# One layer on one core: keys' and values' compression earlier, one more pair of chunks, fewer single chunks under the attentions

## The chip, the core and the metric

The kernel runs on one core of one Trainium2 chip. TensorE (PE) multiplies, its operands loaded by a weight load that overlaps the multiplication (PEld); VectorE (DVE) and ScalarE (ACT) do the elementwise work; GpSimd (POOL) issues some DMAs; SyncE (SP) issues most of them. Each engine takes its instructions in the order of the program. The metric is the device time of one execution: median 1623.22 us of 3 runs before the change (1623.16 to 1623.29).

## The reference

One decoder layer over 256 tokens of width 4096. What is computed, with the sizes:

```python
h = rmsnorm(x, norm_g)                 # 256 x 4096
proj = h @ w_in                        # 4096 x 13872: q,k,v,z of A (2048 each), q of B, 6 x 256 k/v of B, z of B, 48 gates
o_a = dilated_mixture(q_a, k_a, v_a)   # 16 heads of 128; three window/dilation patterns, merged
kc, vc = compress(kc), compress(vc)    # 15 blocks of 32 tokens: gelu((block + pe) @ w1) @ w2, w1 is 4096 x 256
o_b = nsa(q_b, kc, vc, ks, vs, kw, vw, gates)   # 16 heads: compressed, selected and windowed keys
y_a = rmsnorm(o_a, out_g_a) * silu(z_a)
y_b = rmsnorm(o_b, out_g_b) * silu(z_b)
out = rmsnorm(x + concat(y_a, y_b) @ w_out, final_g)
```

All inputs and outputs are 32-bit floats.

## The kernel before

**Products in three parts.** Each 32-bit operand is split into a high and a low part (`split_to`, L102: ACT rounds the high part at L105, DVE subtracts to get the low part at L106), and a product is three matmuls (`mm3`, L97: lines 98, 99, 100; the first needs only the high part of the streamed operand, the second its low part).

**Chunks.** The columns of `w_in` are worked off in chunks of 512. A chunk by itself (`add_chunk`, `run_stream`) is 32 slices of the contraction x 2 halves of the tokens x 3 = 192 matmuls that stream 512 columns; weights come in 8 units of 1 MB (4 for the narrow chunk of 256 columns, 8 smaller ones for that of 304), each split in two halves, and the name of the product is `acc`. **Pairs** (`run_pairs`) work two chunks at once. Of their 16 steps, 9 (`FAST`) form sums of blocks so that 7 block products do in place of 8, 7 do not: 9 x 21 + 7 x 24 = 357 matmuls for a pair in place of 384. The sums cost DVE more (L436 to L443). Results of a pair go through the tiles `parts` and GpSimd's DMAs to scratch tensors in DRAM, where some are accumulated; of the last pair they are kept on the chip and stored once.

**Stages, in order of time.** (1) The first stage: chunk 20 (keys and values to be compressed), the narrow chunk `kw` (256 columns) and the narrow chunk `vg` (304 columns), while `x` is loaded, split and its sums are formed. (2) Nine pairs, the ninth of them `sel` and `za0`; this stage is put out in the order in which it is written. (3) Single chunks: the gates z 1 to 3 of mixer A, 0 to 3 of mixer B, then the first chunk of the output projection; behind these 8 chunks run the compression of keys and of values, the attentions of mixers A and B, gating and the turning of y (`turn_y`). (4) Three pairs of the output projection, then the last chunk and the final norm.

**What sets the order in stages 1 and 3.** The work behind the chunks is a queue of generators, `tasks`. After each contraction slice `run_stream` adds `pace` to a credit (L368, times the chunk's width over 512, at most 2.0) and calls `advance()` once for each whole credit. `hooks[chunk, slice]` put tasks into the queue or issue loads. A scheduler then fixes the order of the instructions on each engine; `[waits ...]` in the pieces below are waits on another engine or a DMA.

**Compression** (`compress`, L833): 4 transposes `pt` (L840), an ACT copy `cT` (L841), two DVE additions `bt` (L853), the split `bhl`, then 32 matmuls `ph` (L875) of 512 columns over `w1` split in 8 groups of 1024 elements (`w1hl`), a small gelu, and the second product (`pk` for keys, `pv` for values).

**Attention of mixer A** (`attend_a`, L636), for each of 4 groups of 4 heads: scores `s`, ACT's exponential, DVE's weighting, transposes `pt`, split `pah`/`pal`, products with the values `po`.

Of the kernel before, what the change touches and what calls it, by code (L numbers as in the profile page):

```python
# [18 lines left out]
P = 128  # L19
# [64 lines left out]
def hybrid_trunk(ctx: ExitStack, tc: tile.TileContext, a: dict):  # L84
# [45 lines left out]
    x_raw = {}  # L130

    def load_xT(piece):
        q, half = divmod(piece, 2)
        if half == 0:
            xh.append(big.tile([P, QK, SEQ], F32R, name=f"xh{q}", tag="x", bufs=8))
            xl.append(big.tile([P, QK, SEQ], F32R, name=f"xl{q}", tag="x", bufs=8))
        t = x_raw[piece] = room["o"].tile([P, G4, SEQ], F32, name="xp", tag="o", bufs=8)
# [163 lines left out]
    def run_stream(begin=None, last=False, ordered=None):  # L301
# [7 lines left out]
        for i, (u, s) in enumerate(subs):  # L309
            while True:  # L310
                if n_st < len(units) and n_st <= u + (2 if i else 0):
# [3 lines left out]
                    if first and 8 <= n_st < 12:  # L315
                        load_x_nat(2 * (n_st - 8))
                        load_x_nat(2 * (n_st - 8) + 1)
# [41 lines left out]
            for j in range(n):  # L359
                k = k0 + n * s + j  # L360
                for m in range(NT):
                    h, l = lhs(k, m)
                    mm3(ps[m][:, :width], h, l, wh[:, j], wl[:, j], start=(k == 0), stop=(k == KT - 1))
                if k == KT - 1:
                    done(ps)
                if (c, k) in hooks:
                    hooks[c, k]()
                credit = min(credit + pace * width / CW, 2.0)  # L368
                while credit >= 1.0 and tasks:
                    credit -= 1.0  # L370
                    advance()
# [347 lines left out]
    waiting, finished, gated = [("a", 0)], set(), set()  # L719
# [9 lines left out]
    def mixer_done(which):  # L729
# [4 lines left out]
        todo = list(waiting)  # L734
        waiting.clear()
# [13 lines left out]
        while loaded:  # L749
            z, sz = loaded.popleft()  # L750
            for m in range(NT):
                nc.scalar.activation(sz[m], sz[m], AF.Silu, scale=rstd[:, m : m + 1] if z == ("a", 0) else 1.0)
# [80 lines left out]
    def compress(t, which):  # L833

        tT = room["zq"].tile([P, 2, NT, P], F32, name="cT", tag="zt", bufs=4)
# [20 lines left out]
        split_to(w2h, w2l, w2)  # L856
        yield
        ph = room["pso"].tile([4 * NC, 2, HID], F32, name="ph", tag="po")
        ready = {}
        for grp in range(9):  # L860
            if grp < 8:
                w = room["work"].tile([P, 2, 4, HID], F32R, name="w1hl", tag="n", bufs=2)
                hs = slice(4 * (grp % 2), 4 * (grp % 2) + 4)
                split_to(w[:, 0], w[:, 1], w1[4 * which + grp // 2][:, hs])
                ready[grp] = w
                if grp % 2 == 1:
                    load_w1(4 * which + grp // 2 + 3)
                if grp == 4 and which == 0:
                    load_small(1)
# [32 lines left out]
        if which == 0:  # L902
# [4 lines left out]
            kc = room["work"].tile([P, 2, CP], F32, name="kc", tag="kc", bufs=1)  # L907
# [3 lines left out]
        else:  # L911
            for g in range(2):
                wide = room["zq"].tile([P, 2, 3, Q], F32, name="wide", tag="zt", bufs=4)
# [3 lines left out]
                rh = room["work"].tile([P, 2, 3 * Q], F32R, name="rh", tag="pTh", bufs=2)  # L917
                rl = room["work"].tile([P, 2, 3 * Q], F32R, name="rl", tag="pTl", bufs=2)
# [360 lines left out]
    dcs.append(((21, 12), ("sel", "za0")))  # L1279
    ordered = ExitStack()  # L1280
# [45 lines left out]
    hooks[0, 3] = load_first  # L1326
    hooks[0, 8] = lambda: load_w1(2)
# [7 lines left out]
    hooks[n_in - 1, 16] = lambda: tasks.extend(turn_y("a", f) for f in range(8, 16, 2))  # L1335
# [121 lines left out]
```

## Time and profile before

| | us |
|---|---|
| median of 3 runs | 1623.22 |
| the profiled execution, its own time | 1622.32 |
| its span, first to last instruction | 1620.5 |
| PE busy in it | 1601.9 (99%) |
| DVE busy | 1368.8 (84%) |
| ACT busy | 994.6 (61%) |
| DMA moved, mean | 384.87 MB, 237 GB/s |

The profile's page says what share of the span each engine was busy, the chain of waits says what the last instruction was waiting for, step by step back; a table by stretch (start:end in us from the span's start) says the same of a stage, with the clock granted to TensorE (1.00 is its upper level of 2.4 GHz, 0.50 is 1.2 GHz) and the share of time in which the DMA engines moved data. Matmuls overlap, so what one costs is the distance of two starts and not the duration in a row.

### The profile page before, as it was taken

How to read it: one execution, taken by the hardware profiler on the slowest of the kernel's cores; microseconds unless marked ns; L12 is line 12 of the kernel's file. 1: busy time of each engine (PE TensorE's matmuls, PEld its weight loads, DVE VectorE, ACT ScalarE, POOL GpSimd, SP SyncE). 2: the span in 40 equal slices, each digit the busy share in tenths (PEclk: the TensorE clock that was granted, in tenths of full speed). 3: DMA queues.
4: the chain of work that ended last, by engine and by line, in shares of the span. 5: the costliest groups of instructions: out<-in, count | busy, mean ns of one | idle time of the engine just before them, and what ended most of it. 6: DMA issues, size and time to landing. Idle time of an engine off the chain costs nothing.

```text
span 1620.5 us, 20719 instructions
## 1 busy us (share of the span) xinstructions
PE 1601.9 (99%) x7685; PEld 1326.4 (82%) x7685; DVE 1368.8 (84%) x1596; ACT 994.6 (61%) x1242; POOL 142.6 (9%) x196
## 2 busy tenths in 40 slices
PE   9999999999999999999999999999999999999997
PEld 6998888888888888888887788888888887888887
DVE  8679989898999898989878877788788779989885
ACT  7755656565656565656546666766667655656553
POOL 0000212021212020202000000000000000202110
PEclk9999999999999999999999999999999999999999
DMA  8776888888888888888888555654345556988874
GB/s 336 268 250 208 261 264 260 254 260 266 256 270 259 253 263 262 264 249 262 251 312 306 179 190 193 233 174 143 117 144 189 179 194 211 261 252 259 280 299 169
DMA packets 104565, 384.87 MB, mean 237 GB/s; under 512 B 12496, under 2 KB 13136, under 8 KB 93072
## 3 DMA queue, kind: packets, MB, share of 16 engines
q1 hardware_dynamic: 81792, 332.42, 58.3%
q0 software_dynamic: 22240, 50.08, 13.8%
q8 instruction: 60, 0.98, 0.2%
q10 hardware_dynamic: 432, 1.05, 0.2%
q14 instruction: 41, 0.34, 0.1%
HBM read 334.69 MB, written 50.91 MB: 238 GB/s over the span
## 4 chain that ended last, share of the span: by engine, by line
PE 89%; DVE 6%; issue 2%; DMA 2%; ACT 1%; SPq 0%; ACTq 0%; POOLq 0%; POOL 0%; DVEq 0%
PE p L99 16%; PE p L100 16%; PE p L98 16%; PE acc L99 9%; PE acc L100 9%; PE acc L98 9%; PE e L100 2%; PE e L98 2%; PE e L99 2%; PE ph L875 1%; DVE wl L106 1%; PE pt L1056 1%; DVE bf L443 1%; DMA w<-in_w_in 1%; DVE bp L106 1%
## 5 line engine op out<-in xcount | busy, mean ns | idle before, releaser
L106 DVE TENSOR_TENSOR wl<-w,wh 128x1024 fp32r<-128x1024 f32 (+2 forms) x178 | 207.7, 1171 | 99.4 <-ACT wh L105 98.9
L105 ACT ACTIVATE wh<-w 128x1024 fp32r<-128x1024 f32 (+2 forms) x178 | 180.4, 1017 | 115.3 <-PE acc L100 99.9
L98 PE MATMUL acc<-wh,xh 128*128 128x512 f32 (+2 forms) x640 | 242.7, 379 | 0.6 <-ACT wh L105 0.6
L443 DVE TENSOR_TENSOR bf<-bt,bf 128x2048 fp32r<-128x2048 f32 x106 | 242.1, 2284 | 0.0
L99 PE MATMUL acc<-wl,xh 128*128 128x512 f32 (+2 forms) x640 | 239.7, 375 | 1.3 <-DVE wl L106 1.3
L100 PE MATMUL acc<-wh,xl 128*128 128x512 f32 (+2 forms) x640 | 239.2, 374 | 0.0
L106 DVE TENSOR_TENSOR bp<-bw,bp 128x2048 fp32r<-128x2048 f32 x72 | 164.8, 2288 | 69.5 <-ACT bp L105 69.5
L438 ACT ACTIVATE bf<-bt 128x1024 fp32r<-128x1024 f32 x106 | 112.4, 1060 | 163.0 <-DVE bt L436 162.6
L435 ACT ACTIVATE bf<-bw 128x1536 fp32r<-128x1536 f32 x106 | 157.7, 1488 | 72.2 <-DMA bw<-in_w_in 39.4
L105 ACT ACTIVATE bp<-bw 128x2048 fp32r<-128x2048 f32 x72 | 137.6, 1911 | 94.1 <-PE e L100 78.2
L442 DVE TENSOR_TENSOR bf<-bw,bf 128x1536 fp32r<-128x1536 f32 x106 | 185.6, 1751 | 0.0
L436 DVE TENSOR_TENSOR bt<-bw 128x1024 f32<-128x1024 f32 x106 | 129.5, 1222 | 12.6 <-DMA bw<-in_w_in 7.0
L441 ACT ACTIVATE bf<-bt 128x1024 fp32r<-128x1024 f32 x106 | 112.7, 1063 | 41.8 <-DVE bt L440 38.7
L99 PEld LDWEIGHTS acc<-wl,xh 128*128 128x128 f32 x640 | 120.6, 188 | 20.1 <-DVE wl L106 3.0
L100 PEld LDWEIGHTS acc<-wh,xl 128*128 128x128 f32 x640 | 120.2, 188 | 20.4
L98 PEld LDWEIGHTS acc<-wh,xh 128*128 128x128 f32 x640 | 120.4, 188 | 18.9 <-ACT wh L105 1.1
L98 PE MATMUL p<-bp,xh 128*128 128x512 f32 x324 | 126.0, 389 | 0.0
L99 PE MATMUL p<-bp,xh 128*128 128x512 f32 x324 | 126.0, 389 | 0.0
L100 PE MATMUL p<-bp,xl 128*128 128x512 f32 x324 | 126.0, 389 | 0.0
L99 PE MATMUL p<-bf,sum 128*128 128x512 f32 x320 | 124.7, 390 | 0.0
L98 PE MATMUL p<-bf,sum 128*128 128x512 f32 x320 | 124.6, 390 | 0.0
L100 PE MATMUL p<-bf,sum 128*128 128x512 f32 x320 | 124.5, 389 | 0.0
(327 smaller groups left out, 3373.8 us busy)
## 6 DMA issues: line engine op xcount, KB each, us to landing
bw<-in_w_in SPq DMA_DIRECT2D x288, 512.0 KB, 6.5
w<-in_w_in SPq DMA_DIRECT2D x60, 1024.0 KB, 5.2
bw<-in_w_out SPq DMA_DIRECT2D x96, 512.0 KB, 5.6
w<-in_w_out SPq DMA_DIRECT2D x16, 1024.0 KB, 5.5
scr_q<-parts POOLq DMA_DIRECT2D x30, 256.0 KB, 7.8
scr_k<-parts POOLq DMA_DIRECT2D x30, 256.0 KB, 7.7
scr_v<-parts POOLq DMA_DIRECT2D x30, 256.0 KB, 7.9
scr_qb<-parts POOLq DMA_DIRECT2D x30, 256.0 KB, 8.3
```

The costliest lines, as they stand in the source:

```text
L98: nc.tensor.matmul(out, lh, rh, start=start, stop=False)
L99: nc.tensor.matmul(out, lh, rl, start=False, stop=False)
L100: nc.tensor.matmul(out, ll, rh, start=False, stop=stop)
L105: nc.scalar.activation(h, src, AF.Copy)
L106: nc.vector.tensor_sub(l, src, h.bitcast(F32))
L435: nc.scalar.activation(h[:, :3], w[:, B22:], AF.Copy)
L436: nc.vector.tensor_tensor(t[:, T3 : T1 + 1], w[:, B22 : B11 + 1], w[:, B12 : B12 + 1].to_broadcast([P, 2, CW]), op=OP.subtract)
L438: nc.scalar.activation(h[:, 3:5], t[:, T3 : T1 + 1], AF.Copy)
L441: nc.scalar.activation(h[:, 5:], t[:, T2:], AF.Copy)
L442: nc.vector.tensor_sub(l[:, :3], w[:, B22:], h[:, :3].bitcast(F32))
L443: nc.vector.tensor_sub(l[:, 3:], t, h[:, 3:].bitcast(F32))
L875: nc.tensor.matmul(ph, both, w[:, :, j], start=l == 0, stop=l == CBL - 1)
```

## The change

Three things move together. (a) The compression of keys and values runs behind the two narrow chunks of the first stage in place of the first chunks of stage 3: the chunk's result `kvc` stays on the chip, the loads of `w1` and of `x` in its natural layout come earlier, `w1` is split in 16 groups of 512 elements in place of 8 of 1024, and its tiles share the buffers of `x`'s (`tag="xn"`, 4 of them). (b) The gates `za1` and `za2` become a tenth pair, so `sel` and `za0` go through the accumulating scratch and `za1`, `za2` are what the last pair keeps. (c) The attentions start at slice 6 of the first of 6 single chunks (5 gates and the first of the output projection) with `pace` 1.7 in place of 1.1 and 1.5, the credit's ceiling is 3.0, and `turn_y` of mixer A goes to the front of the queue.

```diff
@@ load_xT: one tile for two pieces, 4 buffers @@
+            x_pair[q] = room["o"].tile([P, 2, G4, SEQ], F32, name="xp", tag="o", bufs=4)
+        t = x_raw[piece] = x_pair[q][:, half]
@@ split_unit and run_stream: x in its natural layout two units earlier @@
-        if room["first"] and 8 <= u < 12:
-            square_x(2 * (u - 8) + half)
+        if room["first"] and 8 <= u < 10:
+            for i in range(2):
+                square_x(4 * (u - 8) + 2 * half + i)
-                    if first and 8 <= n_st < 12:
+                    if first and 6 <= n_st < 10:
-                credit = min(credit + pace * width / CW, 2.0)
+                credit = min(credit + pace * width / CW, 3.0)
@@ gates @@
+    paired = [("a", i) for i in range(3)]
-    waiting, finished, gated = [("a", 0)], set(), set()
+    waiting, finished, gated = list(paired), set(), set()
@@ compress: buffers, groups of half the size @@
-        tT = room["zq"].tile([P, 2, NT, P], F32, name="cT", tag="zt", bufs=4)
+        tT = room["work"].tile([P, 2, NT, P], F32, name="cT", tag="st")
-        for grp in range(9):
-            if grp < 8:
-                w = room["work"].tile([P, 2, 4, HID], F32R, name="w1hl", tag="n", bufs=2)
+        for grp in range(17):
+            if grp < 16:
+                w = spare([P, 2, 2, HID], F32R, "w1hl")
...
+            if grp % 2:
+                yield
...
-                rh = room["work"].tile([P, 2, 3 * Q], F32R, name="rh", tag="pTh", bufs=2)
-                rl = room["work"].tile([P, 2, 3 * Q], F32R, name="rl", tag="pTl", bufs=2)
+                r = spare([P, 2, 2, 3 * Q], F32R, "rhl")
@@ first stage @@
-    add_chunk([a["w_kw"][g] for g in range(4)], 2 * HD, x_lhs, evict_away("kw", 2 * HD), pace=0.8)
-    add_chunk([a["w_vg"][g] for g in range(8)], 2 * HD + NGATE, x_lhs, last_ps.extend, pace=0.8)
+    add_chunk([a["w_kw"][g] for g in range(4)], 2 * HD, x_lhs, evict_away("kw", 2 * HD), pace=1.4)
+    add_chunk([a["w_vg"][g] for g in range(8)], 2 * HD + NGATE, x_lhs, last_ps.extend, pace=1.6)
+
+    def start_compression():
+        kvc = room["ev"].tile([P, NT, CW], F32, name="kvc", tag="ev", bufs=3)
+        for m in range(NT):
+            nc.scalar.activation(kvc[:, m], first_ps[m], AF.Copy, scale=rstd[:, m : m + 1])
+        tasks.extend([compress(kvc, 0), compress(kvc, 1)])
-    hooks[1, 26] = token_rms
-    hooks[1, 28] = lambda: evict_away("kvc")(first_ps)
+    for k, i in ((2, 0), (6, 1), (10, 2)):
+        hooks[1, k] = lambda i=i: load_w1(i)
+    hooks[1, 4] = lambda: load_small(0)
+    hooks[1, 14] = token_rms
+    hooks[1, 16] = start_compression
@@ pairs and stage 3 @@
     dcs.append(((21, 12), ("sel", "za0")))
+    dcs.append(((13, 14), ("za1", "za2")))
-        tasks.extend([compress(t, 0), compress(t, 1)] + [attend_a(hg) for hg in range(4)] + [mixer_done("a"), start_b()]
+        tasks.extend([attend_a(hg) for hg in range(4)] + [mixer_done("a"), start_b()]
-    hooks[0, 10] = attentions
-    z_chunks = [("a", 12, i) for i in range(1, 4)] + [("b", 22, i) for i in range(4)]
+    hooks[0, 6] = attentions
+    z_chunks = [("a", 12, 3)] + [("b", 22, i) for i in range(4)]
-        add_chunk(w_chunk(c + i), CW, x_lhs, gate_z(which, i), pace=1.5 if chunks else 1.1)
+        add_chunk(w_chunk(c + i), CW, x_lhs, gate_z(which, i), pace=1.7)
-    hooks[n_in - 1, 8] = lambda: tasks.extend(turn_y("a", f) for f in range(0, 8, 2))
+    hooks[n_in - 1, 8] = lambda: tasks.extendleft(turn_y("a", f) for f in range(0, 8, 2))
```

**First place: the start of the values' compression.** On DVE before, in stage 3 (names: `bt` block sums, `bhl` their split, `wl` low parts of a chunk's weights, `w1hl` split `w1`):

```order
L853 TENSOR_TENSOR bt<-cT,pe 128x480 x2
L106 TENSOR_TENSOR wl<-w,wh 128x1024
L106 TENSOR_TENSOR bhl<-bt,bhl 128x32x30
L570 TENSOR_SCALAR fetched<-fetched,rstd 128x512 x2
L106 TENSOR_TENSOR wl<-w,wh 128x1024
L106 TENSOR_TENSOR w1hl<-w_6013,w1hl 128x1024 x2
```

And now, behind the chunk `vg`:

```order
L858 TENSOR_TENSOR bt<-cT,pe 128x480 x2
L106 TENSOR_TENSOR w2hl<-w_792,w2hl 128x256
L106 TENSOR_TENSOR w1hl<-w_867,w1hl 128x512 x2
L106 TENSOR_TENSOR bhl<-bt,bhl 128x32x30
L106 TENSOR_TENSOR wl<-w,wh 128x608 x2
L106 TENSOR_TENSOR w1hl<-w_867,w1hl 128x512 x2
```

The split of `bhl` now stands behind three splits of compression weights, and the chunk's own low parts stand behind it. On PE at the same place, the last rows between the transposes `pt` and the first `ph` after the change:

```order
L100 MATMUL acc<-wh,xl_109 128x304
L98 MATMUL acc<-wh,xh_108 128x304
L99 MATMUL acc<-wl,xh_108 128x304
L100 MATMUL acc<-wh,xl_109 128x304
L98 MATMUL acc<-wh,xh_170 128x304 x2
L880 MATMUL ph<-w1hl,bhl 60x512 x4
L99 MATMUL acc<-wl,xh_170 128x304
```

Between the 4 transposes `pt` and the first `ph` there stand 14 matmuls of 304 columns now, and 22 of 512 columns before; for the keys it is 46 of 256 columns now.

**Second place: the first pair's weights on SP.** Before (names: `w` units of `vg`, `bw` raw blocks of the pairs, `scr` scratch):

```order
L255 DMA w<-in_w_vg 128x1216 [waits DMAHW3_49,DVE_49]
L255 DMA w<-in_w_vg 128x1216 [waits DMAHW5_49,DVE_49]
L428 DMA bw_1150<-in_w_in 128x1024 [waits DMAHW1_49]
L429 DMA bw_1150<-in_w_in 128x1024
L428 DMA bw_1151<-in_w_in 128x1024
L429 DMA bw_1151<-in_w_in 128x1024 [waits DMAHW4_49]
```

And now:

```order
L828 DMA w_1121<-in_cmp_v_w 128x2048 [waits DVE_49]
L256 DMA w<-in_w_vg 128x1216 [waits DMAHW2_49,DMAHW6_49,DVE_49,Activation_49]
L256 DMA w<-in_w_vg 128x1216 [waits DMAHW7_49,DMAHW3_49,DVE_49]
L430 DMA bw_1451<-in_w_in 128x1024 [waits DMAHW4_49,DVE_49,PE_49]
L431 DMA bw_1451<-in_w_in 128x1024
L430 DMA bw_1452<-in_w_in 128x1024 [waits Pool_49]
```

The first load of the pairs waits for PE and DVE now: its place in the memory was the last `rhl` of the values' compression, and what it waits for is the last `pv` matmul and that tile's split. Behind that `pv` there stand 55 matmuls of `vg`.

**Third place: turning y of mixer A on PE.** Before, in the last gate chunk, the 4 turns (4 transposes each) stand in this way:

```order
L783 MATMUL pt<-ident,o_a_6482 128x128 x8
L98 MATMUL acc<-wh,xh_168 128x512
L99 MATMUL acc<-wl,xh_168 128x512
L100 MATMUL acc<-wh,xl_169 128x512
L98 MATMUL acc<-wh,xh_168 128x512
L99 MATMUL acc<-wl,xh_168 128x512
L100 MATMUL acc<-wh,xl_169 128x512
L783 MATMUL pt<-ident,o_a_6482 128x128 x4
```

And now, inside the last head group of mixer B:

```order
L1063 MATMUL pt<-ident,nb 128x128 x4
L786 MATMUL pt<-ident,o_a_6745 128x128 x4
L99 MATMUL acc<-wl,xh_170 128x512
L100 MATMUL acc<-wh,xl_171 128x512
L1082 MATMUL po<-pbh,vc_75 128x512
L786 MATMUL pt<-ident,o_a_6745 128x128 x12
L98 MATMUL po<-pbh,vB 128x512
L1063 MATMUL pt<-ident,nb 128x128 x4
```

Three turns follow each other with nothing between, on the three banks of `pt`.

## Rows read from the trace of the kernel before

**Rows 1.** The page: busy time of each engine; shares of the chain of waits.
```profile
PE 1601.9 (99%) x7685; PEld 1326.4 (82%) x7685; DVE 1368.8 (84%) x1596; ACT 994.6 (61%) x1242; POOL 142.6 (9%) x196
PE 89%; DVE 6%; issue 2%; DMA 2%; ACT 1%; SPq 0%; ACTq 0%; POOLq 0%; POOL 0%; DVEq 0%
```

**Rows 2.** Busy time by stretch: chunk 20, kw, vg, first pair, mixer A, later.
```profile
core 0: us, PE busy (x) PEld busy (x) DVE busy (x) ACT busy (x) POOL busy (x), PEclk, DMA share, GB/s
7.20:53.60 46.40, 45.79 (x192) 35.96 (x193) 44.99 (x89) 39.18 (x70) 0.00 (x0) 1.00 0.93 359
53.60:76.10 22.50, 22.50 (x193) 22.49 (x192) 12.45 (x19) 16.12 (x25) 0.70 (x1) 1.00 0.67 240
76.10:103.00 26.90, 26.90 (x194) 26.90 (x193) 13.36 (x16) 14.39 (x19) 0.00 (x0) 1.00 0.71 242
103.00:184.00 81.00, 81.00 (x359) 67.02 (x358) 75.24 (x54) 49.07 (x43) 2.78 (x5) 1.00 0.67 225
943.50:975.90 32.40, 31.49 (x176) 26.41 (x174) 25.00 (x58) 21.63 (x40) 0.00 (x0) 1.00 0.55 191
1010.00:1220.00 210.00, 209.19 (x1093) 171.04 (x1092) 171.37 (x417) 139.65 (x304) 4.40 (x10) 1.00 0.46 160
```

**Rows 3.** PE in order of time: first matmuls of the pairs and of stage 3.
```profile
103.03 0.40 PE L98 MATMUL p<-bf,xh 128*128 128x512 f32 x1
...
832.44 0.39 PE L98 MATMUL acc<-wh,xh 128*128 128x512 f32 x1
```

**Rows 4.** PE's waits: total us, times, longest us.
```profile
PE s L98 <- DVE pal L106: 2.8, 4, 1.1
PE acc L99 <- DVE wl L106: 1.3, 2, 0.7
```

**Rows 5.** The values' compression before, on PE, ACT and DVE (start us, us).
```profile
877.09 0.27 PE L840 MATMUL pt<-ident,fetched 128*128 128x128 f32 x1
...
877.73 0.60 ACT L841 ACTIVATE cT<-pt 128x512 f32<-128x512 f32 x1 [0.94 <-PE pt L840]
...
880.32 1.03 ACT L105 ACTIVATE bhl<-bt 128x960 fp32r<-128x960 f32 x1
...
878.36 1.93 DVE L853 TENSOR_TENSOR bt<-cT,pe 128x480 f32<-128x480 f32 x2 [0.37 <-ACT cT L841]
...
881.42 1.15 DVE L106 TENSOR_TENSOR bhl<-bt,bhl 128x960 fp32r<-128x960 f32 x1
...
882.72 1.11 PE L875 MATMUL ph<-w1hl,bhl 128*60 128x512 f32 x4
```

**Rows 6.** Splits of 512 and 256 elements on DVE (start us, us).
```profile
31.56 0.68 DVE L106 TENSOR_TENSOR sum<-st,sum 128x512 fp32r<-128x512 f32 x1
...
834.97 0.42 DVE L106 TENSOR_TENSOR w2l<-w,w2h 128x256 fp32r<-128x256 f32 x1 [1.65 <-ACT w2h L105]
```

**Rows 7.** The first pair's weights: issue, us to landing, first split.
```profile
90.06 0.42 SPq L428 DMA_DIRECT2D bw<-in_w_in  x1
90.53 0.43 SPq L429 DMA_DIRECT2D bw<-in_w_in  x1
...
bw<-in_w_in SPq DMA_DIRECT2D x2, 512.0 KB, 5.4
...
98.81 1.90 ACT L105 ACTIVATE bf<-bw 128x2048 fp32r<-128x2048 f32 x1
...
100.74 2.29 DVE L106 TENSOR_TENSOR bf<-bw,bf 128x2048 fp32r<-128x2048 f32 x1 [1.01 <-ACT bf L105]
```

**Rows 8.** ACT's copies of turned y: ns min/median/max.
```profile
L787 ACT ACTIVATE o_a<-pt,g_out x16: 466/484/511, 1232.9 to 1250.6; 128x256 f32<-128x256 f32 x16
```

**Rows 9.** The end of the span by stretch; the warm-up matmuls at its start.
```profile
1604.00:1613.00 9.00, 5.54 (x47) 5.34 (x45) 2.68 (x9) 1.67 (x3) 0.55 (x1) 1.00 0.31 123
1614.00:1620.00 6.00, 0.00 (x0) 0.00 (x0) 0.00 (x0) 0.00 (x0) 0.00 (x0) 0.50 0.68 267
...
1.26 5.30 PE L297 MATMUL warm<-idle 128*128 128x512 bf16 x13 [1.26 <-DVE idle L294]
```

More of the change, by code (lines that the diff above doesn't have):

```diff
@@ L128, in hybrid_trunk @@
     xh, xl = [], []
-    x_raw = {}
+    x_raw, x_pair = {}, {}
     def load_xT(piece):
@@ L314, in run_stream @@
                     stage_unit(n_st)
[L315 to L317 removed]
+                    if first and 6 <= n_st < 10:
+                        load_x_nat(2 * (n_st - 6))
+                        load_x_nat(2 * (n_st - 6) + 1)
                     n_st += 1
@@ L733, in mixer_done @@
         loaded = deque()
-        todo = list(waiting)
-        waiting.clear()
+        todo = [z for z in waiting if z[0] in finished]
+        waiting[:] = [z for z in waiting if z not in todo]
         def load():
@@ L751, in mixer_done @@
             for m in range(NT):
-                nc.scalar.activation(sz[m], sz[m], AF.Silu, scale=rstd[:, m : m + 1] if z == ("a", 0) else 1.0)
+                nc.scalar.activation(sz[m], sz[m], AF.Silu, scale=rstd[:, m : m + 1] if z in paired else 1.0)
             yield
@@ L806, in sum_y @@
         yield
-    B = {}
+    B = {
+        "kch": cst.tile([P, 2, CP], F32R, name="kch"),
+        "kcl": cst.tile([P, 2, CP], F32R, name="kcl"),
+        "vc3": cst.tile([3 * Q, 2, HD], F32R, name="vc3"),
+    }
     def open_b():
         B["gates"] = room["work"].tile([P, NT, NGATE], F32, name="gates", bufs=1)
-        B["kch"] = room["work"].tile([P, 2, CP], F32R, name="kch", bufs=1)
-        B["kcl"] = room["work"].tile([P, 2, CP], F32R, name="kcl", bufs=1)
-        B["vc3"] = room["work"].tile([3 * Q, 2, HD], F32R, name="vc3", bufs=1)
     w1, small = {}, {}
@@ L826, in load_small @@
     def load_small(which):
-        pe = room["work"].tile([P, CBL], F32, name="pe", tag="pe", bufs=2)
+        pe = room["work"].tile([P, CBL], F32, name="pe", tag="pe")
         nc.sync.dma_start(pe, a[f"cmp_{'kv'[which]}_pe"])
-        w2 = room["zq"].tile([P, 2, HD], F32, name="w2", tag="zt", bufs=4)
+        w2 = room["work"].tile([P, 2, HID // 2], F32, name="w2", tag="a22")
         nc.sync.dma_start(w2, a[f"cmp_{'kv'[which]}_w2"])
@@ L833, in compress, with spare @@
     def compress(t, which):
-        tT = room["zq"].tile([P, 2, NT, P], F32, name="cT", tag="zt", bufs=4)
+        def spare(shape, dt, name):
+            return room["work"].tile(shape, dt, name=name, tag="xn", bufs=4)
+        tT = room["work"].tile([P, 2, NT, P], F32, name="cT", tag="st")
         pt = room["psm"].tile([P, 2, NT, P], F32, name="pt", tag="ps")
@@ L841, in compress @@
         nc.scalar.activation(tT, pt, AF.Copy)
-        if which == 1:
-            st["va"], st["qa"] = fetch("v0"), fetch("q0")
         pe, w2 = small.pop(which)
-        w2h = room["work"].tile([P, 2, HD], F32R, name="w2h", tag="pTh", bufs=2)
-        w2l = room["work"].tile([P, 2, HD], F32R, name="w2l", tag="pTl", bufs=2)
+        w2hl = room["work"].tile([P, 2, 2, HD], F32R, name="w2hl", tag="st")
+        w2h, w2l = w2hl[:, 0], w2hl[:, 1]
         yield
         bhl = room["o"].tile([P, CBL, 2, 2, NC], F32R, name="bhl", tag="o", bufs=4)
-        bt = room["work"].tile([P, CBL, 2, NC], F32, name="bt", tag="qTh", bufs=1)
+        bt = spare([P, CBL, 2, NC], F32, "bt")
         toks = tT.rearrange("p g m t -> p g (m t)").rearrange("p g (c b) -> p b g c", b=CST)
@@ L856, in compress @@
         split_to(w2h, w2l, w2)
+        if which == 0:
+            load_small(1)
         yield
@@ L859, in compress @@
         ready = {}
-        for grp in range(9):
-            if grp < 8:
-                w = room["work"].tile([P, 2, 4, HID], F32R, name="w1hl", tag="n", bufs=2)
-                hs = slice(4 * (grp % 2), 4 * (grp % 2) + 4)
-                split_to(w[:, 0], w[:, 1], w1[4 * which + grp // 2][:, hs])
+        for grp in range(17):
+            if grp < 16:
+                w = spare([P, 2, 2, HID], F32R, "w1hl")
+                hs = slice(2 * (grp % 4), 2 * (grp % 4) + 2)
+                split_to(w[:, 0], w[:, 1], w1[4 * which + grp // 4][:, hs])
                 ready[grp] = w
[L866 to L869, printed above, removed]
+                if grp % 4 == 3:
+                    load_w1(4 * which + grp // 4 + 3)
             if grp > 0:
                 w = ready.pop(grp - 1)
-                for j in range(4):
-                    l = (grp - 1) * 4 + j
+                for j in range(2):
+                    l = (grp - 1) * 2 + j
                     both = bhl[:, l].rearrange("p s g c -> p (s g c)")
                     nc.tensor.matmul(ph, both, w[:, :, j], start=l == 0, stop=l == CBL - 1)
-            yield
-        halves = room["work"].tile([4 * NC, HID], F32, name="halves", tag="pTh", bufs=2)
+            if grp % 2:
+                yield
+        yield
+        halves = spare([4 * NC, HID], F32, "halves")
         nc.scalar.activation(halves, ph[:, 0], AF.Copy)
@@ L906, in compress @@
                     start=hf == 0, stop=hf == 1)
-            kc = room["work"].tile([P, 2, CP], F32, name="kc", tag="kc", bufs=1)
+            kc = spare([P, 2, CP], F32, "kc")
             nc.gpsimd.memset(kc, 0.0)
```

17 lines of the change are left out of this document (6 added, 11 removed).

## The prediction

> **What bounds the kernel now.** I read the page's shares first, then the chain of waits, the table by stretch, PE's list of waits, and last the rows at the places where the change puts something.
>
> TensorE is busy 99% of the span and carries 89% of the chain; DVE is at 84%, ACT at 61% [rows 1]. So time goes when PE has fewer instructions, and comes when PE has to wait. What an instruction costs there is read from stretches in which PE never pauses: chunk `kw` has 192 matmuls in 22.50 us, 0.117 each; `vg` 192 in 26.90, 0.140 each [rows 2]; the nine pairs run from 103.03 to 832.44, 9 x 357 = 3213 matmuls, 0.227 each and 81.0 us a pair [rows 3]. PE's list of waits is short: 2.8 us for low parts of mixer A's weights, 1.3 for low parts of a chunk's weights [rows 4]. None names a product of the compression, so before the change both compressions cost PE nothing but their own matmuls.
>
> The reader is also to see how near DVE is: 75.24 of 81.00 in a pair, 25.00 of 32.40 (77%) in a head group of mixer A, 171.4 of 210.0 (82%) in mixer B, but only 12.45 of 22.50 and 13.36 of 26.90 behind the narrow chunks [rows 2]. That last slack is where the change puts the compression.
>
> **The change part by part**, against the profiled execution's own 1622.3 us (0.9 under the median of the runs).
>
> *The tenth pair.* Two single chunks of 192 matmuls become a pair of 357: 27 fewer, 27 x 0.227 = **-6.1**.
>
> *The start of stage 3.* One of the two waits for `wl`, 0.7 at its longest [rows 4], stands at the first matmuls of stage 3, where before the change `w1`'s first loads and splits come. Nothing of that is ahead of the chunk after the change: **-0.7**. What is late next there is the chunk's own first weights, loaded far ahead: 0.
>
> *The compression, moved.* Its 64 `ph` and its small products cost PE the same wherever they stand, some 14.5 us for the `ph`: 0. What counts is whether PE waits for them. Before, for the values, the chain from the first `pt` to the first `ph` is 877.09 to 882.72, 5.6 us: transposes 0.64, `cT` 0.60, the two `bt` 1.93, `bhl` on ACT 1.03 and on DVE 1.15 [rows 5]. In its cover stood 22 matmuls of the chunk, 22 x 0.227 = 5.0, and the transposes.
>
> Now DVE's order has `w2hl` (0.42) and splits of 512 (0.68 each [rows 6]) between `bt` and `bhl`. Up to the end of `bt` it is 3.2 us. Keys: 0.42 + 3 x 0.68 + 1.15 = 3.6 more, 6.8 in all; cover: transposes 0.44 and 46 matmuls of `kw`, 46 x 0.117 = 5.4, so 5.8: PE waits about 1.0, less if the first splits fit in while `cT` is made; I take **+0.6** (0 to 1.5). Values: 0.42 + 2 x 0.68 + 1.15 = 2.9 more, 6.1 in all; cover 0.44 + 14 x 0.140 = 2.4. PE waits 3.7, and since DVE has other splits ready to fill its own gaps, **+3.4** (2.5 to 4.0). Behind the waiting `ph` stand all further matmuls of `vg`.
>
> *DVE beside PE while `ph` runs.* A slice of `kw` is 6 x 0.117 = 0.70 on PE and earns 0.7 of a step; a step is 4 `ph`, 0.91, and two splits, 1.36 on DVE. So 1.34 a slice on PE, and on DVE 0.95 for these and 12.45 / 32 = 0.39 for `wl`: 1.34. For `vg` it is 1.70 on PE, and on DVE 1.29 + 13.36 / 32 = 1.71 [rows 2, 6]. The two are level: DVE can't catch up while a compression runs, and what it starts late stays late. I take **+0.6** (0 to 3).
>
> *The small functions behind the `ph`* (`halves`, gelu, `pk`, `pv`): a dozen small steps on DVE and ACT between chunk slices, as before: **+0.4** (0 to 1.5).
>
> *The first pair's weights.* Before, SP issued them at 90.06, 13 us ahead of their use, and only the free buffer held them [rows 7]. Now they wait for the last `pv`. From there: the second half's issue 0.47, landing 5.4, ACT 1.90, DVE 2.29, together 10.1 [rows 7]. Behind that `pv` stand 55 matmuls of `vg`, 55 x 0.140 = 7.7. So 2.4 would show, less if the load lands faster with fewer transfers beside it; the pair's first matmul needs only ACT's part. I take **+1.6** (0.5 to 3). All of the pairs' loads stand behind it on SP, but in a pair the DMA engines move data for 0.67 of the time [rows 2], so the later ones catch up.
>
> *DMA in the first stage.* 8.4 MB of `w1` and `w2` come into it. From 53.6 to 103.0 there move 22.50 x 240 + 26.90 x 242 = 11.9 MB; with 8.4 more over some 70 us that is 290 GB/s, and chunk 20 shows 359 [rows 2]. **0** (0 to 2, if `vg`'s units come late). `x`'s squares two units earlier put a few us more on ACT in chunk 20, at 39.18 of 46.40 [rows 2]: 0 (0 to 1.4).
>
> *Denser attentions.* In mixer A a head group stands beside 84 matmuls of a chunk in place of 96: 12 x 0.227 = 2.7 less PE work to hide the same chain of scores, exponential and splits. Its stretch goes from 32.4 to about 29, and DVE's part from 25.0 to 23.8 (one split of 1024 fewer, about 1.2 by the 1.15 for 960 in `bhl` [rows 5]), 82%. The waits for `pal`, 2.8 us in 4 [rows 4], grow somewhat: **+1.0** (-0.5 to +4). In mixer B, pace 1.7 for 1.5, DVE goes from 82% to some 84%: within the same bounds.
>
> *Turning y.* Three turns now stand in a row on PE; each needs two ACT copies of 0.48 [rows 8] before its bank is free, so the third and fourth can wait about 1 us each, if ACT isn't busy with the exponentials. **+0.5** (0 to 2.5).
>
> Sum: -6.1 - 0.7 + 0.6 + 3.4 + 0.6 + 0.4 + 1.6 + 1.0 + 0.5 = +1.3. 1622.3 + 1.3 = 1623.6, on the scale of the median **1624.5**: the 27 matmuls saved are given back as waits, above all at the start of the values' compression.
>
> **The rivals.**
>
> *Faster: the waits aren't there.* If DVE gets the values' first splits done ahead of `bt`, if the pair's first load lands in 3 us, and if mixers A and B hide their chains as before, only -6.8 and some 0.8 of small waits are left: 1616.3, on the median's scale 1617.2. For it: before, no wait of PE names the compression [rows 4], and the engines have more free time behind `kw` and `vg` than anywhere [rows 2]. Against it: the cover of 2.4 stands against a chain that took 5.6 in the same form [rows 5].
>
> *Slower: DVE decides under the attentions.* The pair and the higher pace take 4 x 2.7 = 10.8 us of chunk work away from mixer A alone. If the chain from score to score is what lasts there, and not PE's work, that time comes back as waits `s<-pal`. Half of it back, in place of my +1.0: 1623.6 - 1.0 + 5.4 = 1628.0, median 1628.9; all of it 1634.3. It makes the kernel slower by more than measurement can tell from no change (about 0.2%, 3.2 us) as soon as some 3 us of the 10.8 come back beside the waits above. For it: the only wait repeated in every head group names exactly this. Against it: it is 0.7 a group, in 32 us.
>
> *The clock falls after the wait.* At the span's end PE does nothing for 3.5 of 9.0 us and is granted 1.00 still; from 1614, with no work at all, 0.50 [rows 9]. A wait of 3.4 to 3.7 at the values' start lies at that edge. The 13 warm-up matmuls take 5.30 us, 0.41 each, against 0.227 at the upper level [rows 3, 9], so such a fall would cost about 13 x 0.18 = 2.4: 1626.9. The rows don't show a fall inside the kernel, though chunks stop for up to 1.1 us.
>
> The Trainium skill (TensorE: Matmul & The Clock Gate, "HAM oscillation — how this bites in real kernels") says that a gap in PE's work can throttle the engine again, so that what follows starts cold; by that rule the time would be this rival's. The trace agrees only with the fall at the end; no row shows it behind so short a wait.
>
> **How the numbers follow.** Forecast 44%, faster rival 28%, slower rival 24%, the clock 4%. The forecast's own range, with not all of the bounds on one side, is 1620.5 to 1628. The range that leaves out 2 in 10 reaches to the faster rival's middle and to the slower one's half: 1617 to 1630. Faster by over 0.2% (under 1620.0): the faster rival and a small part of the forecast, 0.30. Slower by over 0.2% (over 1626.5): the slower rival, the clock and a seventh of the forecast less a part of the rival, 0.30. Within: 0.40.
>
> **What would show it.** In PE's list of waits: `ph` on DVE's `bhl` once with 2.5 to 4 us (values) and once with up to 1.5 (keys); the first pair's `p` on `bf` with 0.5 to 3, and SP's first `bw` waiting for PE; none at the start of stage 3. The pairs still 81.0 apart, ten of them. `s<-pal` at 3 to 5 us in all; `pt` of the turns on `o_a` up to 2.5. Wrong it is if the `ph` waits are under 1 us together (then the faster rival), if waits inside the attentions pass 6 us (then the slower one), if a stretch between 76 and 120 shows a granted clock under 1.00, or if the pair's distance changes.

## The result, and the profile after

The changed kernel takes 1635.64 us (median of 4 runs, 1634.46 to 1636.42) against 1623.19: 1.0077 of the time before, 95% interval 1.0059 to 1.0094. It is slower by 12.4 us, where 1624.5 was forecast and the range ended at 1630. The profiled execution took 1635.77 with a span of 1634.0, 13.5 more than before.

The page, the shares of the engines and of the chain of waits, answers to [rows 1]:

```profile
PE 1605.4 (98%) x7658; PEld 1327.0 (81%) x7658; DVE 1401.1 (86%) x1632; ACT 1011.0 (62%) x1266; POOL 154.6 (9%) x211
PE 83%; DVE 7%; DMA 5%; issue 2%; ACT 2%; SPq 0%; ACTq 0%; POOLq 0%; POOL 0%; DVEq 0%
```

PE's busy time rose although it has 27 matmuls fewer. PE's waits (total us, times, longest us), against [rows 4]:

```profile
PE acc L99 <- DVE wl L106: 3.8, 3, 3.3
PE acc L98 <- ACT wh L105: 3.3, 2, 3.1
PE p L99 <- DVE bf L106: 1.6, 1, 1.6
PE pt L682 <- DVE n L672: 1.5, 2, 0.9
PE s L98 <- DVE pal L106: 1.4, 2, 0.9
...
PE p L98 <- ACT away L579: 1.2, 1, 1.2
...
PE ph L880 <- DVE bhl L106: 0.5, 1, 0.5
```

The table by stretch (us, then PE, PEld, DVE, ACT and POOL busy, granted clock, DMA share, GB/s) for three places, each with the stretch behind it:

```profile
92.00:100.00 8.00, 4.93 (x26) 4.16 (x25) 7.45 (x11) 6.86 (x12) 0.00 (x0) 0.88 0.20 60
...
128.60:138.50 9.90, 7.12 (x20) 5.12 (x19) 7.60 (x6) 5.91 (x6) 0.00 (x0) 0.68 0.86 291
138.50:219.50 81.00, 81.00 (x357) 66.93 (x356) 72.59 (x52) 48.66 (x42) 4.99 (x7) 1.00 0.67 221
945.00:957.00 12.00, 9.55 (x43) 7.56 (x41) 4.96 (x11) 4.52 (x5) 1.97 (x4) 1.00 0.77 283
957.00:962.00 5.00, 4.18 (x13) 3.40 (x14) 3.50 (x4) 0.60 (x1) 0.00 (x0) 0.66 0.61 205
```

There are three stops, and behind each the granted clock is below 1.00, where before it was 1.00 in every stretch shown but the last [rows 2, 9]. The matmuls there last longer, which is the larger part of why PE's busy time rose (the sum is below). The pair behind the second stop takes 81.0 us as ever.

**First stop, the values' start.** PE, then ACT, in order of time (start us, us, instruction, idle before and what ended it):

```profile
93.27 0.30 PE L100 MATMUL acc<-wh,xl 128*128 128x304 f32 x1
96.64 0.55 PE L98 MATMUL acc<-wh,xh 128*128 128x304 f32 x2 [3.07 <-ACT wh L105]
...
98.80 0.46 PE L100 MATMUL acc<-wh,xl 128*128 128x304 f32 x1
```

```profile
94.47 1.01 ACT L105 ACTIVATE bhl<-bt 128x960 fp32r<-128x960 f32 x1 [0.61 <-DVE bt L858]
...
95.90 1.29 ACT L105 ACTIVATE wh<-w 128x608 fp32r<-128x608 f32 x2
```

PE does not wait for `ph`, but for high parts of the chunk's own weights: on ACT they stand behind `bhl`, which waits for DVE's `bt`. The wait that was forecast stood right behind it, on DVE and then PE:

```profile
95.89 1.15 DVE L106 TENSOR_TENSOR bhl<-bt,bhl 128x960 fp32r<-128x960 f32 x1
```

```profile
97.09 1.15 PE L880 MATMUL ph<-w1hl,bhl 128*60 128x512 f32 x4
```

`bhl` was ready at 97.04, so even with `wh` in time PE would have stopped at `ph` for about as long (an estimate from these rows). The 304-column matmuls behind the stop last 0.46 in place of 0.30.

**Second stop, the first pair.** PE, and then ACT:

```profile
128.63 0.40 PE L98 MATMUL p<-bf,xh 128*128 128x512 f32 x1
130.65 0.50 PE L99 MATMUL p<-bf,xh 128*128 128x512 f32 x1 [1.61 <-DVE bf L106]
...
133.25 0.80 PE L98 MATMUL p<-bf,xh 128*128 128x512 f32 x1 [1.17 <-ACT away L579]
133.84 0.63 PE L99 MATMUL p<-bf,xh 128*128 128x512 f32 x1
```

```profile
130.88 1.91 ACT L105 ACTIVATE bp<-bw 128x2048 fp32r<-128x2048 f32 x1 [2.61 <-DMA bw<-in_w_in]
132.70 0.90 ACT L579 ACTIVATE away<-acc,rstd 128x304 f32<-128x304 f32 x2
```

SP issued the first block's load behind the last `pv`:

```profile
121.07 0.33 SPq L430 DMA_DIRECT2D bw<-in_w_in  x1
```

The late first block costs 1.61. The second block is late too, `away` (which empties two PSUM banks that the pair needs) stands behind its split on ACT, and that costs 1.17 more. From 133.84 on a matmul lasts 0.63 in place of 0.39 [rows 3].

**Third stop, the first chunk of stage 3.** DVE, and then PE:

```profile
952.60 0.18 DVE L940 CAST kTh<-kch 128x32 fp32r<-128x32 f32 x1 [3.35 <-DMA scr_za<-parts]
...
955.75 0.88 DVE L572 TENSOR_SCALAR fetched<-fetched,rstd 128x512 f32<-128x512 f32 x2 [2.87 <-DMA fetched<-scr_k]
956.55 3.49 DVE L106 TENSOR_TENSOR wl<-w,wh 128x1024 fp32r<-128x1024 f32 x3
```

```profile
957.82 0.50 PE L99 MATMUL acc<-wl,xh 128*128 128x512 f32 x1 [3.28 <-DVE wl L106]
...
958.53 0.63 PE L98 MATMUL acc<-wh,xh 128*128 128x512 f32 x1
```

The scaling of the first head group's keys stands on DVE ahead of the chunk's low parts and waits for its load, which SP could issue only when a buffer of the values was free (948.48). DVE's wait ahead of that, 3.35 for a store of the last pair, did not stop PE by itself: e1 below has it too (2.46), and PE runs on there.

**The sum.** Stops of over 0.05 us, from 10 us on: 16.4 us in all, 5.6 before: +10.8. Distances of starts above 0.227 (512 columns) and 0.140 (304) behind the three stops: 1.8, 2.8 and some 1.7 (the last estimated from 10 distances, as transposes stand among them): +6.3. 27 matmuls fewer: -6.1. Together +11.0 of the 13.5; the other 2.5 us are spread over many small distances and are not settled.

### The profile page after: what moved, and what is told of

Its sections match the earlier page's. It is cut to its first block, busy times and chain, and to the rows that moved or that the text cites. A ratio compares the mean times of both kernels' runs of the same rounds, so it can differ in the third digit from the quotient of the medians.

```text
span 1634.0 us, 20792 instructions
## 1 busy us (share of the span) xinstructions
PE 1605.4 (98%) x7658; PEld 1327.0 (81%) x7658; DVE 1401.1 (86%) x1632; ACT 1011.0 (62%) x1266; POOL 154.6 (9%) x211
## 4 chain that ended last, share of the span: by engine, by line
PE 83%; DVE 7%; DMA 5%; issue 2%; ACT 2%; SPq 0%; ACTq 0%; POOLq 0%; POOL 0%; DVEq 0%
PE p L99 17%; PE p L100 17%; PE p L98 17%; PE acc L99 7%; PE acc L100 6%; PE acc L98 6%; DMA bw<-in_w_in 2%; PE e L98 2%; PE e L100 2%; PE e L99 2%; DVE bf L445 1%; PE ph L880 1%; PE pt L1063 1%; DVE bf L444 1%; DVE wl L106 1%
## 5 line engine op out<-in xcount | busy, mean ns | idle before, releaser
L445 DVE TENSOR_TENSOR bf<-bt,bf 128x2048 fp32r<-128x2048 f32 x115 | 262.7, 2284 | 0.0
L106 DVE TENSOR_TENSOR wl<-w,wh 128x1024 fp32r<-128x1024 f32 (+2 forms) x146 | 168.2, 1159 | 51.9 <-ACT wh L105 51.4
L105 ACT ACTIVATE wh<-w 128x1024 fp32r<-128x1024 f32 (+2 forms) x146 | 146.5, 1008 | 80.2 <-PE acc L100 66.3
L98 PE MATMUL acc<-wh,xh 128*128 128x512 f32 (+2 forms) x512 | 192.1, 378 | 3.4 <-ACT wh L105 3.3
L99 PE MATMUL acc<-wl,xh 128*128 128x512 f32 (+2 forms) x512 | 191.0, 373 | 4.0 <-DVE wl L106 3.8
L100 PE MATMUL acc<-wh,xl 128*128 128x512 f32 (+2 forms) x512 | 190.2, 372 | 0.0
L98 PE MATMUL p<-bp,xh 128*128 128x512 f32 x360 | 140.0, 389 | 0.0
L99 PE MATMUL p<-bp,xh 128*128 128x512 f32 x360 | 140.0, 389 | 0.0
L99 PE MATMUL p<-bf,sum 128*128 128x512 f32 x356 | 138.7, 389 | 0.7 <-DVE bf L445 0.7
L98 PE MATMUL p<-bf,sum 128*128 128x512 f32 x356 | 138.7, 390 | 0.0
L100 PE MATMUL p<-bf,sum 128*128 128x512 f32 x356 | 138.6, 389 | 0.0
L99 PE MATMUL p<-bf,xh 128*128 128x512 f32 x333 | 130.6, 392 | 1.6 <-DVE bf L106 1.6
L98 PE MATMUL p<-bf,xh 128*128 128x512 f32 x333 | 130.7, 392 | 1.2 <-ACT away L579 1.2
L100 PE MATMUL p<-bf,xl 128*128 128x512 f32 x333 | 130.5, 392 | 0.0
```

What stands on the lines that cost most here:

```text
L98: nc.tensor.matmul(out, lh, rh, start=start, stop=False)
L99: nc.tensor.matmul(out, lh, rl, start=False, stop=False)
L100: nc.tensor.matmul(out, ll, rh, start=False, stop=stop)
L105: nc.scalar.activation(h, src, AF.Copy)
L106: nc.vector.tensor_sub(l, src, h.bitcast(F32))
L445: nc.vector.tensor_sub(l[:, 3:], t, h[:, 3:].bitcast(F32))
```

## The experiments

My theory after the result: the loss is these three stops, each dearer than its length because of the clock behind it. Rivals: the denser attentions, or a compression that is bound by DVE.

**e1: the first keys' load early.** The third stop's cause alone.

```diff
-        ksrc = fetch(f"k{hg}")
+        ksrc = st.pop("k0") if hg == 0 else fetch(f"k{hg}")
 def load_first():
     st["va"], st["qa"] = fetch("v0"), fetch("q0")
+    st["k0"] = room["o"].tile([P, NT, CW], F32, name="fetched", tag="o", bufs=4)
+    nc.sync.dma_start(st["k0"], scratch("k0"))
```

> The changed kernel with one edit: the first head group's keys are fetched in slice 1 of stage 3 into a buffer of their own, in place of behind the values' split. In the changed kernel's trace DVE stood until 955.75 before the scaling of these keys, the chunk's low parts `wl` behind it, and PE waited 3.28 us, after which about 4 us ran at the granted clock 0.50 (1.7 us more by the distances of the starts). Theory (PE's three stops, each with the clock behind it): this wait goes and the clock stays at 1.00 there: 1635.6 - 3.3 - 1.7 = 1630.6. Rival (the clock does not hang on this stop): 1632.3. Rival (the loss is in the denser attentions as a whole, and this wait is made up for later): 1635.6.

Measured: 1630.65, 1.0041 of before (1.0028 to 1.0053). The table by stretch, of the first chunk of stage 3:

```profile
944.00:955.00 11.00, 11.00 (x52) 9.05 (x51) 7.68 (x13) 5.12 (x6) 0.96 (x2) 1.00 0.98 344
955.00:965.00 10.00, 10.00 (x57) 8.23 (x55) 6.51 (x11) 4.75 (x7) 0.00 (x0) 1.00 0.88 334
```

No stop, and no fall of the clock there; the time is 5.0 lower, more than the wait of 3.28. That the rest is the clock behind this one stop is not shown, though the 1630.6 expected by that reading was met: in this profile the first pair's stop is still there (1.74 and 0.87), but the clock stayed up behind it as well:

```profile
126.00:145.00 19.00, 16.39 (x82) 13.63 (x81) 13.82 (x11) 10.56 (x9) 0.00 (x0) 1.00 0.91 293
```

So two falls of the clock are gone here, and some of that came back elsewhere (`s` on `kaT`, for one, waits 1.1 in place of 0.7).

**e2: `rhl` in other memory.** The second stop's cause alone.

```diff
-                wide = spare([P, 2, 3, Q], F32, "wide")
+                wide = room["o"].tile([P, 2, 3, Q], F32, name="wide", tag="o", bufs=4)
-                r = spare([P, 2, 2, 3 * Q], F32R, "rhl")
+                r = room["o"].tile([P, 2, 2, 3 * Q], F32R, name="rhl", tag="o", bufs=4)
```

> The changed kernel with one edit: the last split of the values' compression (`rhl`, and `wide` ahead of it) lies in other memory than the pairs' first raw block, so that block's load no longer waits for the last `pv` but for work 7 us earlier. In the changed kernel's trace the load was issued at 121.07, PE waited 1.61 and 1.17 us at the first pair, and 13 matmuls behind that ran at the lower clock, 3.3 us more. Theory (stops with the clock behind them): the load is issued at about 114, both waits go and the clock stays up: 1635.6 - 2.8 - 3.3 = 1629.5. Rival (only the waits return): 1632.8. Rival (the load is slow because of the DMA traffic, not because it starts late): 1635 to 1636.

Measured: 1630.19, 1.0041 (1.0029 to 1.0054). SP's first load of the pairs, and the stretch that had a clock of 0.68:

```profile
113.84 0.33 SPq L430 DMA_DIRECT2D bw<-in_w_in  x1
```

```profile
128.60:138.50 9.90, 9.90 (x46) 8.20 (x45) 9.80 (x8) 5.64 (x6) 0.00 (x0) 1.00 0.87 297
```

46 matmul records where there were 20. Without two waits of 2.8 us together the time is 5.4 lower. The 3.3 expected for the clock was too much: the distances above give 2.8, which makes 1630.0. The trace also has a stop of 2.0 at the end of mixer A that the changed kernel's profile does not have, and a lower clock behind it:

```profile
1090.00:1093.00 3.00, 0.98 (x5) 0.52 (x4) 2.23 (x3) 2.87 (x4) 0.00 (x0) 1.00 0.80 335
1093.00:1097.00 4.00, 4.00 (x13) 3.14 (x13) 4.00 (x7) 2.12 (x4) 0.00 (x0) 0.59 0.57 207
```

Other waits are smaller in return (`pt` on `n` 0.6 in place of 1.5, `s` on `kaT` none in place of 0.7). So the 5.4, too, is a net of more than the two waits and their clock.

**e3: the values' front beside the keys' tail, in written order; e4: with e1 and e2.** `compress(t, 1)` is stepped from inside the keys' gelu, and the scheduler is off from the first slice of `vg`.

```diff
+        head = compress(t, 1) if which == 0 else iter(range(9))
+        next(head)
         yield
         halves = ...
+        next(head)
         yield
 ...
+    hooks[2, 0] = lambda: ordered.enter_context(tc.manual_schedule())
```

> The changed kernel with one edit: the front of the values' compression (transposes, block sums, their split) runs beside the tail of the keys' compression, and the chunk `vg` and what lies behind it stand in the order in which they are written. In the changed kernel's trace PE waited 3.07 us for `wh`, which stood on ACT behind `bhl`, and then 18 matmuls ran at the lower clock, 1.8 us more. Theory: wait and clock go, 1635.6 - 3.1 - 1.8 = 1630.7; since the compression ends earlier too, a part of the first pair's waits (up to 6.1) goes with them: 1625 to 1631. Rival (compression behind the narrow chunks is bound by DVE, 1.71 us a slice against PE's 1.70, so that a wait avoided here comes back at later slices): 1634 to 1636.

> The changed kernel with all three edits (keys of the first head group early, `rhl` in other memory, the front of the values' compression ahead). Theory: nothing is left of the three stops and of the clock behind them: 1635.6 - 5.0 - 6.1 - 4.9 = 1619.6, below the kernel before (1623.2) by 0.2%. Rival (the denser attentions and the compression's place cost the rest): the three edits give back less than 12 us and it stays above 1623.2. No stretch should show a granted clock below 1.00 but for the start and the end.

Measured: 1642.51 (1.0119, 1.0105 to 1.0133) and 1636.19 (1.0081, 1.0067 to 1.0095): both missed. PE's waits in e3:

```profile
PE pv L98 <- ACT rhl L105: 4.5, 2, 2.8
...
PE ph L883 <- DVE w1hl L106: 3.1, 1, 3.1
PE ph L883 <- DVE bhl L106: 2.8, 1, 2.8
```

The written order puts `pv` right behind the split it needs, and the turning of the values now stood on ACT ahead of the keys' `bhl`. One stop became four, of 10.4 us together. The wait for `wh` is down to 0.2, but with these in its place the runs do not show what the first stop cost.

**e5: e1 and e2 together.**

> The changed kernel with the two edits that gave back time: first head group's keys early, `rhl` in other memory; the values' start is left as it is. Theory (the stops and the clock behind them are independent and add): 1635.6 - 5.0 - 5.4 (measured each: 1630.65, 1630.19) = 1625.2, still 2 us above the kernel before, with the values' stop (3.1, and 1.6 to 1.8 of clock) left as the largest. Rival (the two overlap, or a wait removed returns in the attentions): 1627.5 to 1630.

Measured: 1626.28, 1.0012 (1.0003 to 1.0021). The two add to within 1.1 us. Its profile shows the first stop as it was, and this behind it:

```profile
96.56 0.55 PE L98 MATMUL acc<-wh,xh 128*128 128x304 f32 x2 [3.09 <-ACT wh L105]
...
97.98 0.30 PE L99 MATMUL acc<-wl,xh 128*128 128x304 f32 x1
```

The matmuls last 0.30: in this execution the clock did not fall behind the same stop that cost 1.8 us more in the changed kernel's.

**e6: the values' front beside the keys' tail, order left to the scheduler, with e1 and e2.**

> The two edits and the front of the values' compression beside the tail of the keys', this time with the order left to the scheduler, so that 31 matmuls of the chunk stand between the turning of the keys' halves and the first product of the values. Theory: the stop of 3.1 shrinks to 0 to 1.5 and the clock stays up: 1625.2 - 4.9 + (0 to 1.5) = 1620.3 to 1621.8, below the kernel before (1623.2) by 0.1 to 0.2%. Rival (DVE is level with PE there, so that a stop of 2.5 us or more, with its clock, comes at another instruction): 1625 or more.

Measured: 1624.63, 1.0003 (0.9994 to 1.0012). The values' start had no stop any more, but the scheduler put the values' `cT` ahead of the keys' `bhl` on ACT, and the keys' start stopped for 2.83:

```profile
73.84 0.60 ACT L848 ACTIVATE cT<-pt 128x512 f32<-128x512 f32 x1 [3.48 <-PE pt L847]
74.33 1.00 ACT L105 ACTIVATE bhl<-bt 128x960 fp32r<-128x960 f32 x1
```

So the stop that the rival named came, for another reason (ACT's order; DVE itself stood idle there, for 2.76), and the time lies just under the rival's 1625.

**e8: as e6, with the values' `cT` in a buffer that `w1hl` must leave first.**

```diff
-        tT = room["work"].tile([P, 2, NT, P], F32, name="cT", tag="st")
+        tT = spare([P, 2, NT, P], F32, "cT") if which else room["work"].tile([P, 2, NT, P], F32, name="cT", tag="st")
```

> The keys' fetch, `rhl` in other memory, and the front of the values' compression beside the tail of the keys', now with `cT` of the values in one of the buffers that `w1hl` leaves free, so that it can't be put ahead of the keys' block sums (in the kernel e6_three_again it was, and the keys' start stopped for 2.8 us). Theory: no stop over 1 us in the first stage: the two-edit kernel's 1626.3 less the values' stop of 3.1 and, where the clock fell behind it, up to 1.8: 1622.0 to 1623.2, level with or just below the kernel before (1623.2 to 1623.6). Rival (DVE and PE are level behind the narrow chunks, so a stop of 2 us or more comes elsewhere): 1625 to 1627.

Measured: 1620.22, 0.998 (0.9971 to 0.9988), below what was expected. The first stage by stretch:

```profile
53.30:76.10 22.80, 22.80 (x179) 21.34 (x179) 17.58 (x23) 18.63 (x31) 0.70 (x1) 1.00 0.77 300
76.10:123.00 46.90, 46.53 (x302) 40.71 (x301) 38.56 (x78) 32.63 (x60) 0.13 (x1) 1.00 0.72 268
```

PE is busy for all but 0.37 us, with DVE at 82% behind `vg`: the compression fits behind the narrow chunks, at a clock of 1.00, and a compression bound by DVE falls as the cause. The step from e5 is 6.1, more than the stop of 3.1 with up to 1.8 of clock; the rest is not settled.

**e7 and e9: without the tenth pair.** 8 single chunks and the old pace; e7 is otherwise the changed kernel, e9 has e8's repairs. The main lines (the turns of y and the scratch of the last pair go back to the kernel before as well):

```diff
-    dcs.append(((13, 14), ("za1", "za2")))
-    z_chunks = [("a", 12, 3)] + [("b", 22, i) for i in range(4)]
+    z_chunks = [("a", 12, i) for i in range(1, 4)] + [("b", 22, i) for i in range(4)]
-    hooks[0, 6] = attentions
+    hooks[0, 10] = attentions
-        add_chunk(w_chunk(c + i), CW, x_lhs, gate_z(which, i), pace=1.7)
+        add_chunk(w_chunk(c + i), CW, x_lhs, gate_z(which, i), pace=1.5 if chunks else 1.1)
-                credit = min(credit + pace * width / CW, 3.0)
+                credit = min(credit + pace * width / CW, 2.0)
```

> The changed kernel without its tenth pair and its denser attentions: single chunks, order and pace of stage 3 as in the kernel before (8 chunks, attentions from slice 10, pace 1.1 and 1.5, turns of y at the end of the queue); only the compression stays behind the narrow chunks. Theory (the loss is made by the compression's new place: 4.9 for the values' start, 0.5 for the keys', 6.1 for the first pair's loads, about 1 for dearer products): 1623.2 + 12.5 - 0.7 = 1635; with the stop at the start of stage 3 there too, up to 1640. Rival (the tenth pair and the density cost what the first stage doesn't): 1625 to 1630, and the tenth pair then makes things worse.

> The same kernel without the tenth pair and the denser attentions (8 single chunks, attentions from slice 10, pace 1.1 and 1.5). It measures what the pair and the density bring together, with all large stops gone from both. Theory (27 matmuls at 0.227 bring 6.1, the density gives back 1.5 to 2.5 in the attentions): 3.5 to 4.5 more than e8_values_front, 1626 to 1627.5. Rival (the density gives back half of the 10.8 us or more, as the prediction's slower rival had it): less than 1 us more than e8_values_front, or even less time than it.

Measured: 1638.03 (1.0084, 1.007 to 1.0098) and 1620.9 (0.9986, 0.9977 to 0.9995). e7 is as expected: the compression's new place alone makes the loss, with the stop at stage 3's start there too (`acc` on `wl`, 3.7 at the longest). e9 is not: the repaired compression alone is faster than before by 2.3 us, and the tenth pair and the density together add 0.7, which the two intervals do not tell from nothing, not 3.5 to 4.5. Part of the 2.3 stands in mixer A: PE's waits from stage 3's start to 1110 are 1.4 in e9, 3.5 in the kernel before. Waits of mixer A (854 to 1110) in e9, and in e8 (933 to 1110):

```profile
PE pt L682 <- DVE n L672: 1.4, 5, 0.5
```

```profile
PE s L98 <- DVE pal L106: 1.5, 2, 1.1
PE pt L682 <- DVE n L672: 1.4, 2, 0.8
PE s L99 <- DVE kaT L106: 0.7, 1, 0.7
PE acc L99 <- DVE wl L106: 0.5, 1, 0.5
```

This spoke for the density: what the pair brought seemed to return as waits. So the density was varied by itself.

**e10 and e11: only the pace of stage 3, 1.55 and 2.2 in place of e8's 1.7.**

> The kernel e8_values_front with the attentions thinner: pace 1.55 in place of 1.7 in stage 3, so that they last until the end of the fifth gate chunk (half chunks with 73 to 100 other matmuls in place of 82 to 111). Theory (how dense the attentions stand decides what they cost, 5 us between 1.1 to 1.5 with 8 chunks and 1.7 with 6): about 1 us less, 1618.7 to 1620. Rival (what the tenth pair loses lies in the six chunks as such, not in the density): 1620.2 as at 1.7, within 0.5.

> The same with pace 2.2: half chunks with up to 126 other matmuls, the attentions done earlier. Theory (density): 2 to 6 us more than e8_values_front, 1622 to 1626. Rival (no effect of the density): 1620.2 within 0.5.

Measured: 1625.17 (1.001, 1.0001 to 1.0019) and 1616.88 (0.9965, 0.9953 to 0.9977). Both are the other way round, and the density as the cause falls. (The kernel before, run beside them, took 1623.61; beside e8 and e9 it took 1623.25.) PE's waits in stage 3, e10 and then e11:

```profile
PE pt L682 <- DVE n L672: 3.3, 4, 1.2
PE acc L98 <- ACT wh L105: 3.2, 1, 3.2
PE pt L786 <- DVE o_b L728: 1.6, 3, 1.2
```

```profile
PE pt L682 <- DVE n L672: 1.8, 3, 1.3
```

At 1.55 mixer B ends so late that its turning runs into the output chunk, which stops for 3.2; at 2.2 the waits are about as in e9 and more of the tenth pair's gain stays: 4.0 under e9. The three paces have different orders of instructions, and I take the order, not how many stand beside a chunk, to decide; no run shows that by itself. Why 1.7 falls worse than 2.2 in mixer A is not settled.

## Why the prediction was wrong, point by point

- **"What is late next there is the chunk's own first weights, loaded far ahead: 0"**: this step failed. It took the compression's splits for all that could stand ahead of the chunk's low parts at the start of stage 3. With them gone the attention's first scaling moved up into their place on DVE and waited for a DMA: +3.3 in place of -0.7. e1, in which those keys are loaded early, has no stop there.
- **"The clock falls after the wait", 4%**: the rival came true beside the forecast, and three times, since it came with any of the three stops and not with the values' alone: +6.3 in place of one fall of 2.4. The forecast's sum had the clock at nothing, and this is the second step that failed. The size is read from the changed kernel's own distances; e1 and e2 fit it (3.28 us of stop less made 5.0, 2.8 less made 5.4) without showing it by themselves. The rival had a wait of 3.4 to 3.7 in view; the stops in front of the three falls were 3.07, 1.61 with 1.17, and 3.28. The Trainium skill's rule (TensorE: Matmul & The Clock Gate, "HAM oscillation — how this bites in real kernels"), that a gap can throttle the engine again, agrees with the granted clock of 0.88, 0.68 and 0.66 behind the three stops; e1's and e5's profiles show that it need not follow.
- **"The first pair's weights", +1.6 (0.5 to 3)**: the term's own wait came out at 1.61, in the way worked out. What was queued behind was left out: the second block was late as well, `away` behind it on ACT, and two PSUM banks with it: 1.17 more.
- **Values' start, +3.4 (2.5 to 4.0)**: the size was right, 3.07, and the chain too, since `bhl` on DVE was ready only at 97.04; but the instruction that waited was another, the chunk's `wh` behind `bhl` on ACT. The rows beside the term named DVE's order alone. **Keys' start, +0.6**: 0.5.
- **"DVE beside PE", +0.6 (0 to 3), and "small functions", +0.4**: at most a few tenths; in e8 PE is busy for 46.53 of 46.90 us.
- **Tenth pair, -6.1**: ten pairs at 81.1, with the stops and the clock taken off: right. **Denser attentions, +1.0, and turning y, +0.5**: the waits up to the end of mixer A other than the third stop are 3.9 in place of 2.8, and no wait names the turns. The size is about right, but by luck: `s` on `pal`, which was to grow from 2.8 to 3 to 5, fell to 1.4, and the rest are waits that the prediction does not name (`pt` on `n` 1.5, `s` on `kaT` 0.7). In the working, 32.4 - 2.7 is 29.7 and not "about 29", so DVE's share would be 80%; nothing else hangs on it. The slower rival did not come either: the time lies beside its full case (1634.3), but by chance, since the waits inside mixer A are 3.9 and the loss lies elsewhere; e11 shows that a higher pace need not cost.
- **Its own signs**: it expected no wait at the start of stage 3, and named a granted clock under 1.00 between 76 and 120 as a sign that it is wrong. The trace shows a wait of 3.28 there and a clock of 0.88. The pair's `p` on `bf` and SP's first `bw` behind the last `pv` came as named. One sign misled: `ph` waits under 1 us together were to speak for the faster rival; they are 0.5, because the stop shows at `wh` in place of `ph`.

So the sum took each stop at its length, and found two of the three. With all three stops and no clock the kernel would have taken about 1629 (1635.6 - 6.3), inside the range.

## What to carry to other kernels

When work is moved away from the start of a stage, look in the new order at what takes its place on each engine ahead of the chunk's own splits, above all an instruction that waits for a load. Here PE was 99% busy, and its stops of about 3 us cost their length and, in some executions, half of it or more again in clock (1.8, 2.8 and 1.7 in the changed kernel's), so three of them outweighed a saving of 6. A move that loses need not be wrong: with three buffers chosen otherwise, the front of the values' compression beside the keys' tail, and a pace of 2.2, the same change is 0.35% faster than the kernel before (e11).

## What the runs showed of the hardware that I had not expected

A stop of PE and the lower clock behind it do not go together in every execution: behind the same stop of 3.07 to 3.09 us the 304-column matmuls lasted 0.46 in the changed kernel's profile and 0.30 in e5's, and the first pair's two waits were followed by a clock of 0.68 there and of 1.00 in e1's. And a stop need not be long to cost: the 2.0 of e2 was followed by a clock of 0.59, while behind a stop of 0.9 in mixer A the changed kernel's clock stayed at 1.00:

```profile
972.00:975.00 3.00, 2.09 (x14) 1.49 (x13) 3.00 (x11) 1.90 (x5) 0.00 (x0) 1.00 0.29 123
975.00:980.00 5.00, 5.00 (x29) 4.26 (x28) 4.96 (x18) 3.58 (x8) 0.00 (x0) 1.00 0.10 16
```
